# A two-layer trunk in emulated fp32: w_up's product by pairs of pieces in seven block products, w_down by two pieces

## The chip, the core and the metric

One core of a Trainium2 chip runs the whole kernel, one launch. The metric is device time in microseconds; the kernel before takes 1413.79 us, the median of 3 runs (1412.65 to 1416.82).

## What is computed

One inference step of a trunk of two layers: 512 tokens of a new stream and 8 x 16 tokens of running streams, 640 rows of width 1024, all in fp32. Each layer has a mixer (trailing means in the first, forgetting attention in the second) beside memory attention, an output projection, and a squared-ReLU MLP of width 4096, each wrapped in RMS norms. The part that the change touches, for both layers:

```python
h = rmsnorm(x, g_mlp_pre)             # (640, 1024)
u = h @ w_up                          # (640, 4096)
a = jnp.square(jax.nn.relu(u))
x = x + rmsnorm(a @ w_down, g_mlp_post)
```

## The kernel before

TensorE multiplies float32r numbers, and fp32 is emulated: a tensor is split into a high part, rounded to float32r, and the remainder, the low part. A product is then three passes: high by high, high by low, low by high. On weights the split is `piece` (L127 to L138): SyncE fetches 128 x 1024 numbers into a raw buffer, ScalarE (ACT) casts them into `wh` (L136), VectorE (DVE) subtracts to give `wl` (L137). In the input projections GpSimd (POOL) first multiplies the raw piece by a gain (L133). Raw buffers come from a ring of 3, the parts from rings of 8.

The 640 tokens are 5 tiles of 128 in two halves of 384 and 256 columns (`HALF`). `proj_fm` (matmuls of L149) gives one piece of w_up's 128 outputs for one half of the tokens: 8 contraction tiles by 3 passes, 24 matmuls, so 48 a piece, half of 384 and half of 256 columns. `activate` puts ReLU and square on ACT and a square and a subtraction (L469, L470) on DVE. `token_major` (L156, L158, L160) multiplies a token tile by w_down's pieces, two banks of 512 columns, 6 matmuls a piece; DVE adds the banks into `y` (L539). The 32 pieces of a layer go in chunks of 4, 2, 4, 4, 4, 4, 4, 6: up for one chunk lies ahead of down for the one before.

Ahead of the MLP, `OutProj` multiplies the mixed columns by w_out tile by tile; `residual` (L411 to L417) takes the RMS norm of a tile (two squares with sums on ACT, a gain on DVE or POOL, L412, then POOL's power, L166, then DVE's L417), `normed` a second one with its own power (L173, L166, L178 or, without a gain, L176). `flush` transposes that tile on PE (L186) and splits it (L189, L190). A layer's last w_down chunk is followed by the same chain for each tile, and at the end of the second layer by `final_tile`, whose last columns are few.

Each engine runs its instructions in a fixed order that a scheduler sets when the program is built, from the order in which the code is written and from priorities (`flush` has a raised one). An instruction that waits holds up all behind it on its engine, and a DMA that SyncE issues waits for the buffer it fills.

## Time and profile before

| what | value |
|---|---|
| runs | 1412.65, 1413.79, 1416.82 us |
| profiled execution, span | 1411.2 us; its own total is not listed beside it |
| PE busy | 1379.7 us, 98% |
| DVE / ACT / POOL busy | 701.5 / 475.3 / 157.1 us |
| mean granted clock of TensorE | 0.993 |
| w_up pieces, w_down pieces | 64 DMAs of 512 KB each |
| mean DMA rate | 119 GB/s |

Busy times are sums over instructions of the execution. An engine that is busy 98% sets the time; what the others do counts where PE waits for it. Times in a timeline are from the span's start.

### The profile page before, as it was taken

How to read it: one execution, taken by the hardware profiler on the slowest of the kernel's cores; microseconds unless marked ns; L12 is line 12 of the kernel's file. 1: busy time of each engine (PE TensorE's matmuls, PEld its weight loads, DVE VectorE, ACT ScalarE, POOL GpSimd, SP SyncE). 2: the span in 40 equal slices, each digit the busy share in tenths (PEclk: the TensorE clock that was granted, in tenths of full speed). 3: DMA queues.
4: the chain of work that ended last, by engine and by line, in shares of the span. 5: the costliest groups of instructions: out<-in, count | busy, mean ns of one | idle time of the engine just before them, and what ended most of it. 6: DMA issues, size and time to landing. Idle time of an engine off the chain costs nothing. (4 is left out here: it accounts for less than half of the span.)

```text
span 1411.2 us, 20878 instructions
## 1 busy us (share of the span) xinstructions
PE 1379.7 (98%) x8496; PEld 1228.2 (87%) x8496; DVE 701.5 (50%) x1230; ACT 475.3 (34%) x917; POOL 157.1 (11%) x148
## 2 busy tenths in 40 slices
PE   7989999999999999999999999999999999999997
PEld 6988879889889899898999886779898989989896
DVE  6556447454435434445735467557453444434434
ACT  6425335223213223133434345345122322213221
POOL 3270000000000000024511212210000000000003
PEclk9999999999999999999999999999999999999999
DMA  7646565222213212122736533735221322213103
GB/s 258 190 91 210 182 222 194 75 90 90 75 45 105 75 60 90 52 98 105 247 119 222 169 117 104 258 128 198 68 87 55 103 66 71 90 32 119 60 1 120
DMA packets 70034, 167.25 MB, mean 119 GB/s; under 512 B 16545, under 2 KB 24225, under 8 KB 69937
## 3 DMA queue, kind: packets, MB, share of 16 engines
q1 hardware_dynamic: 69936, 165.91, 36.2%
q8 instruction: 67, 1.10, 0.3%
q14 instruction: 31, 0.25, 0.1%
HBM read 148.27 MB, written 17.61 MB: 118 GB/s over the span
## 5 line engine op out<-in xcount | busy, mean ns | idle before, releaser
L136 ACT CAST wh<-raw 128x1024 fp32r<-128x1024 f32 (+1 forms) x180 | 188.2, 1046 | 409.6 <-PE b L160 295.7
L137 DVE TENSOR_TENSOR wl<-raw,wh 128x1024 fp32r<-128x1024 f32 (+1 forms) x180 | 227.1, 1265 | 157.7 <-ACT wh L136 157.6
L149 PE MATMUL b<-hhi,wh 128*128 128x256 f32 (+1 forms) x1336 | 228.8, 313 | 5.9 <-DVE memq L563 5.9
L149 PE MATMUL b<-hhi,wl 128*128 128x256 f32 (+1 forms) x1336 | 226.8, 312 | 0.0
L149 PE MATMUL b<-hlo,wh 128*128 128x256 f32 (+1 forms) x1336 | 222.8, 309 | 0.0
L149 PEld LDWEIGHTS b<-hhi,wh 128*128 128x128 f32 x1336 | 205.2, 189 | 9.6 <-DVE memq L563 6.1
L149 PEld LDWEIGHTS b<-hhi,wl 128*128 128x128 f32 x1336 | 205.0, 190 | 0.3
L149 PEld LDWEIGHTS b<-hlo,wh 128*128 128x128 f32 x1336 | 202.8, 189 | 0.0
L158 PE MATMUL b<-wh,ah 128*128 128x512 f32 x628 | 196.2, 393 | 0.0
L156 PE MATMUL b<-wl,ah 128*128 128x512 f32 x628 | 196.1, 393 | 0.0
L160 PE MATMUL b<-wh,al 128*128 128x512 f32 x628 | 196.0, 393 | 0.0
L539 DVE TENSOR_TENSOR y<-y,b 128x512 f32<-128x512 f32 x138 | 88.7, 683 | 174.6 <-PE b L160 174.6
L160 PEld LDWEIGHTS b<-wh,al 128*128 128x128 f32 x628 | 117.9, 188 | 27.5
L158 PEld LDWEIGHTS b<-wh,ah 128*128 128x128 f32 x628 | 117.9, 188 | 26.9
L467 ACT ACTIVATE r<-b 128x384 f32<-128x384 f32 (+1 forms) x128 | 56.1, 438 | 252.1 <-PE b L149 252.1
L156 PEld LDWEIGHTS b<-wl,ah 128*128 128x128 f32 x628 | 116.9, 188 | 25.5
L469 DVE TENSOR_TENSOR r<-r 128x384 f32<-128x384 f32 (+1 forms) x128 | 62.5, 488 | 109.1 <-ACT ah L468 109.1
L133 POOL TENSOR_TENSOR raw<-raw,gfm 128x1024 f32<-128x1024 f32 (+1 forms) x28 | 56.8, 2031 | 475.2 <-DMA raw<-in_w_in 436.2
L412 POOL TENSOR_TENSOR yn<-y,gp 128x512 f32<-128x512 f32 x18 | 23.0, 1297 | 428.7 <-DVE y L539 424.5
L470 DVE TENSOR_TENSOR al<-r,ah 128x384 fp32r<-128x384 f32 (+1 forms) x128 | 62.9, 491 | 4.3
L468 ACT ACTIVATE ah<-r 128x384 fp32r<-128x384 f32 (+1 forms) x128 | 60.4, 472 | 2.1
L156 PE MATMUL b<-wl,cathi 128*128 128x512 f32 x160 | 54.3, 419 | 0.0
(229 smaller groups left out, 1305.5 us busy)
## 6 DMA issues: line engine op xcount, KB each, us to landing
raw<-in_w_up SPq DMA_DIRECT2D x64, 512.0 KB, 3.8
raw<-in_w_down SPq DMA_DIRECT2D x64, 512.0 KB, 3.2
raw<-in_w_in SPq DMA_DIRECT2D x16, 512.0 KB, 4.5
raw<-in_w_out SPq DMA_DIRECT2D x16, 512.0 KB, 3.6
t<-in_cmk SPq DMA_DIRECT2D x32, 256.0 KB, 6.0
t<-in_cmv SPq DMA_DIRECT2D x32, 256.0 KB, 5.0
x<-xr SPq DMA_DIRECT2D x15, 512.0 KB, 2.7
xr<-x SPq DMA_DIRECT2D x15, 512.0 KB, 4.1
```

Of the source, the lines that this page charges most:

```text
L133: nc.gpsimd.tensor_tensor(out=v, in0=v, in1=gain.unsqueeze(2).to_broadcast([P, n, w // n]), op=ALU.mult)
L136: nc.scalar.copy(out=hi[:, :w], in_=raw[:, :w])
L137: nc.vector.tensor_tensor(out=lo[:, :w], in0=raw[:, :w], in1=hi[:, :w].bitcast(F32), op=ALU.subtract)
L149: nc.tensor.matmul(acc[:, :n], w[:, k, :], x[:, k, :], start=(first and k == 0), stop=(last and k == KT - 1))
L156: nc.tensor.matmul(accs[q][:, :nh], xh, lo[:, c[q]], start=first, stop=False)
L158: nc.tensor.matmul(accs[q][:, :nh], xh, hi[:, c[q]], start=False, stop=False)
L160: nc.tensor.matmul(accs[q][:, :nh], xl, hi[:, c[q]], start=False, stop=last)
L467: nc.scalar.activation(out=r, in_=acc[:, :n], func=AF.Relu)
L468: nc.scalar.activation(out=ah, in_=r, func=AF.Square)
L469: nc.vector.tensor_tensor(out=r, in0=r, in1=r, op=ALU.mult)
L470: nc.vector.tensor_tensor(out=al, in0=r, in1=ah.bitcast(F32), op=ALU.subtract)
L539: nc.vector.tensor_tensor(out=yq, in0=yq, in1=accs[q], op=ALU.add)
```

## The change

Pieces of w_up are taken in pairs (16 a layer). The matrix of weights of a pair (1024 contraction rows, 256 outputs) is cut by halves of the contraction, a pair of pieces being the two halves of the outputs, and the tokens are cut into two halves of 320 (`TH`). The product of these 2 x 2 blocks is made of seven block products (`product`, L547, 12 matmuls of 320 columns each) instead of eight. For that, four sums of weight blocks a pair are taken on POOL (L535 to L538) and split into parts by `parts` (L472, L473), and four sums of token blocks are taken once a layer (`other_blocks`, L500 to L507), of which each is split too. The products are put together with adds on DVE (L562) and two copies on ACT (L554, L559). ReLU and square become one instruction on DVE (L584) on 640 columns.

The token sums need all five tiles; so `flush` leaves raw tokens in `hraw` (copies L463, L465), the first two pairs begin with the two products that need only the raw blocks (`head`, `second`), and their remaining five come behind `other_blocks`, with their w_up pieces of the first half fetched a second time (`load(True)`). w_down goes by two pieces, 14 times, and a last time by four. There are 4 raw buffers instead of 3. The gain of the MLP's norm and the pool of its chain are opened behind the last pair.

```diff
-CHUNKS = (4, 2, 4, 4, 4, 4, 4, 6)
+NPAIR = 16
+TH = 320
...
-    wraw = ctx.enter_context(pool("wraw", 3))
+    wraw = ctx.enter_context(pool("wraw", 4))
...
-            if self.late:
-                tile_to(self.hs, *self.late.pop(0))
+            i, xn = self.late.pop(0)
+            with tc.high_priority(offset=HP):
+                for q in range(2):
+                    acc = bank()
+                    for k in range(4):
+                        nc.tensor.transpose(acc[:, k * P:(k + 1) * P], xn[:, (4 * q + k) * P:(4 * q + k + 1) * P], ident)
+                    dst = self.raw[:, 4 * q:4 * q + 4, i * P:(i + 1) * P]
+                    src = acc.rearrange("p (k t) -> p k t", k=4)
+                    if q == 0:
+                        nc.scalar.copy(out=dst, in_=src)
+                    else:
+                        nc.vector.tensor_copy(out=dst, in_=src)
 
...
-    def mlp(l, proj, x_in, cpool, apool, before, finish):
-        hs = proj.hs
...
-            nc.scalar.activation(out=r, in_=acc[:, :n], func=AF.Relu)
-            nc.scalar.activation(out=ah, in_=r, func=AF.Square)
-            pcs = [piece(a["w_up"][l, f]) for f in fs]
-                    acc = proj_fm(pc, hs[t], n)
+    def split(hi, lo, src):
+        nc.scalar.copy(out=hi, in_=src)
+        nc.vector.tensor_tensor(out=lo, in0=src, in1=hi.bitcast(F32), op=ALU.subtract)
+    def mlp(l, proj, x_in, aside, yside, hst, before, finish):
+        hraw = proj.raw
+        ast, tst, yst = ExitStack(), ExitStack(), ExitStack()
+        apool = ast.enter_context(pool(f"act{l}", 1, aside))
+        tpool = tst.enter_context(pool(f"blk{l}", 1, aside))
+        b1 = (hpool.tile([P, KT, TH], F32R, tag="hi0", name=nm("b1h")), hpool.tile([P, KT, TH], F32R, tag="lo0", name=nm("b1l")))
+        b22 = (hpool.tile([P, 4, TH], F32R, tag="hi1", name=nm("b22h")), hpool.tile([P, 4, TH], F32R, tag="lo1", name=nm("b22l")))
+        ts = [(tpool.tile([P, 4, TH], F32R, name=f"t{x}h_{l}"), tpool.tile([P, 4, TH], F32R, name=f"t{x}l_{l}")) for x in range(4)]
+        b11, b21 = ((b1[0][:, 4 * q:4 * q + 4, :], b1[1][:, 4 * q:4 * q + 4, :]) for q in range(2))
+        def first_blocks():
+            for hi, lo, q in ((*b11, 0), (*b21, 1)):
+                split(hi, lo, hraw[:, 4 * q:4 * q + 4, 0:TH])
+        def other_blocks():
+            r11, r21 = (hraw[:, 4 * q:4 * q + 4, 0:TH] for q in range(2))
+            r12, r22 = (hraw[:, 4 * q:4 * q + 4, TH:2 * TH] for q in range(2))
+            nc.vector.tensor_tensor(out=r11, in0=r12, in1=r11, op=ALU.subtract)
+            split(*b22, r22)
+            nc.gpsimd.tensor_tensor(out=r12, in0=r22, in1=r12, op=ALU.subtract)
+            nc.vector.tensor_tensor(out=r22, in0=r22, in1=r11, op=ALU.subtract)
+            split(*ts[1], r22)
+            split(*ts[2], r12)
+            split(*ts[0], r11)
+            nc.vector.tensor_tensor(out=r21, in0=r21, in1=r22, op=ALU.subtract)
+            split(*ts[3], r21)
+        def parts(src, w=D):
+            hi = wring.tile([P, RW], F32R, tag="wh", name=nm("wh"))
+            lo = wring.tile([P, RW], F32R, tag="wl", name=nm("wl"))
+            split(hi[:, :w], lo[:, :w], src)
+            return [(hi[:, 512 * x:512 * x + 512], lo[:, 512 * x:512 * x + 512]) for x in range(2)]
+        class Pair:
+            def __init__(self, c):
+                self.c = c
+                self.r0 = self.fetch(0)
+                self.a11, self.a12 = parts(self.r0[:, :D])
+            def fetch(self, x):
+                raw = wraw.tile([P, RW], F32, tag="raw", name=nm("raw"))
+                nc.sync.dma_start(out=raw[:, :D], in_=a["w_up"][l, 2 * self.c + x])
+                return raw
+            def load(self, again=False):
+                r0 = self.fetch(0) if again else self.r0
+                r1 = self.fetch(1)
+                s = [wraw.tile([P, RW], F32, tag="raw", name=nm("raw")) for _ in range(2)]
+                s1, s2, s3, s4 = (s[x // 2][:, 512 * (x % 2):512 * (x % 2) + 512] for x in range(4))
+                a11, a12, a21, a22 = (r[:, 512 * x:512 * x + 512] for r in (r0, r1) for x in range(2))
+                nc.gpsimd.tensor_tensor(out=s1, in0=a21, in1=a22, op=ALU.add)
+                nc.gpsimd.tensor_tensor(out=s2, in0=s1, in1=a11, op=ALU.subtract)
+                nc.gpsimd.tensor_tensor(out=s3, in0=a11, in1=a21, op=ALU.subtract)
+                nc.gpsimd.tensor_tensor(out=s4, in0=a12, in1=s2, op=ALU.subtract)
+                self.s1, self.s2 = parts(s[0][:, :D])
+                self.s3, self.s4 = parts(s[1][:, :D])
+                self.a22 = parts(a22, 512)[0]
+            def product(self, w, b, acc, first=True, last=True):
+                w = [x.rearrange("p (k m) -> p k m", k=4) for x in w]
+                for wi, bi, f, e in ((0, 0, first, False), (1, 0, False, False), (0, 1, False, last)):
+                    for k in range(4):
+                        nc.tensor.matmul(acc[:, :TH], w[wi][:, k, :], b[bi][:, k, :], start=(f and k == 0), stop=(e and k == 3),
+                                         skip_group_check=not first)
+            def head(self):
+                self.t = apool.tile([P, 2, 2, TH], F32, tag="c", bufs=2, name=nm("c"))
+                acc = long_bank()
+                self.product(self.a11, b11, acc)
+                nc.scalar.copy(out=self.t[:, 0, 1, :], in_=acc[:, :TH])
+                self.x = acc
+            def second(self):
+                self.product(self.a12, b21, self.x, False, True)
+                nc.scalar.copy(out=self.t[:, 0, 0, :], in_=self.x[:, :TH])
+            def add(self, out, in0, acc):
+                nc.vector.tensor_tensor(out=out, in0=in0, in1=acc[:, :TH], op=ALU.add)
+            def middle(self):
+                c12, c21, c22 = self.t[:, 0, 1, :], self.t[:, 1, 0, :], self.t[:, 1, 1, :]
+                y, w, self.z = bank(), bank(), long_bank()
+                self.product(self.s2, ts[1], y)
+                self.add(c12, c12, y)
+                self.product(self.s3, ts[2], w)
+                self.add(c21, c12, w)
+                self.product(self.s1, ts[0], self.z)
+                self.add(c22, c21, self.z)
+            def end(self):
+                c12, c21 = self.t[:, 0, 1, :], self.t[:, 1, 0, :]
+                v = bank()
+                self.product(self.a22, ts[3], v)
+                self.add(c21, c21, v)
+                self.product(self.s4, b22, self.z, False, True)
+                self.add(c12, c12, self.z)
+                out = [None, None]
+                for x in (1, 0):
+                    t = self.t[:, x].rearrange("p h n -> p (h n)")
+                    nc.vector.scalar_tensor_tensor(out=t, in0=t, scalar=0.0, in1=t, op0=ALU.max, op1=ALU.mult)
+                    out[x] = (apool.tile([P, 640], F32R, tag="ah", bufs=4, name=nm("ah")),
+                              apool.tile([P, 640], F32R, tag="al", bufs=4, name=nm("al")))
+                    split(*out[x], t)
+                return out
+            def whole(self):
+                self.load()
+                self.head()
+                self.middle()
+                self.second()
+                return self.end()
...
-        def down(c, tiles):
+        def down(fs, tiles, first, end):
             nf = len(tiles)
-            end = c == len(CHUNKS) - 1
-            pcs = [piece(a["w_down"][l, f]) for f in chunk(c)]
+            pcs = [piece(a["w_down"][l, f]) for f in fs]
             for i in range(NT):
-                if c == 0:
-                    ys.append(apool.tile([P, D], F32, tag=f"y{i}", name=nm(f"y{i}")))
+                if first:
...
-        ready = up(chunk(0), between=proj.flush)
-        for c in range(len(CHUNKS)):
-            nxt = list(chunk(c + 1)) if c + 1 < len(CHUNKS) else []
-            tiles = up(nxt[:1])
-            if c == 1:
-                gpost.append(gain_tile(cpool, a["g_mlp_post"][l], "gp"))
-            down(c, ready)
-            for f in nxt[1:]:
-                tiles = tiles + up([f])
-            ready = tiles
+        pairs = [Pair(0), Pair(1)]
+        first_blocks()
+        for p in pairs:
+            p.head()
+            p.second()
+        proj.flush()
+        other_blocks()
+        hst.close()
+        ypool = yst.enter_context(pool(f"y{l}", 1, yside))
+        ready = []
+        for p in pairs:
+            p.load(True)
+            p.middle()
+            ready.append(p.end())
+        down((0, 1), ready.pop(0), True, False)
+        for c in range(2, NPAIR):
+            ready.append(Pair(c).whole())
+            if c < NPAIR - 1:
+                down((2 * c - 2, 2 * c - 1), ready.pop(0), False, False)
+        tst.close()
+        cpool = ast.enter_context(pool(f"chain{3 + l}", 2, aside))
+        gpost.append(gain_tile(cpool, a["g_mlp_post"][l], "gp"))
+        down(range(2 * NPAIR - 4, 2 * NPAIR), ready[0] + ready[1], False, True)
+        yst.close()
+        return ast
...
-    nc = bacc.Bacc("TRN2", target_bir_lowering=False, num_devices=1)
+    nc = bacc.Bacc("TRN2", target_bir_lowering=False, num_devices=1, dynamic_dma_scratch_size=1024)
```


**Place 1, the start of a layer.** POOL's queue in layer 0 before, from tile 3's two powers and tile 4's two (`s` is one number a row) on:

```order
L166 TENSOR_TENSOR s_384_2135<-s_383_2133,mhalf 128x1
L166 TENSOR_TENSOR s_388_2146<-s_387_2144,mhalf 128x1
L166 TENSOR_TENSOR s_399_2229<-s_398_2227,mhalf 128x1
L166 TENSOR_TENSOR s_403_2240<-s_402_2238,mhalf 128x1
L133 TENSOR_TENSOR raw_5951<-raw_5951,gfm 128x1024
L133 TENSOR_TENSOR raw_5958<-raw_5958,gfm 128x1024
```

and now, from tile 3's first power through both pairs' sums (`raw_2374` and `raw_2375` hold those of pair 0, `raw_2475` and `raw_2476` those of pair 1) up to tile 4's last power:

```order
L167 TENSOR_TENSOR s_380_2131<-s_379_2129,mhalf 128x1
L535 TENSOR_TENSOR raw_2374<-raw_2372 128x512
L536 TENSOR_TENSOR raw_2374<-raw_2374,raw_2370 128x512
L537 TENSOR_TENSOR raw_2375<-raw_2370,raw_2372 128x512
L167 TENSOR_TENSOR s_384_2142<-s_383_2140,mhalf 128x1
L538 TENSOR_TENSOR raw_2375<-raw_2370,raw_2374 128x512
L535 TENSOR_TENSOR raw_2475<-raw_2473 128x512
L536 TENSOR_TENSOR raw_2475<-raw_2475,raw_2471 128x512
L537 TENSOR_TENSOR raw_2476<-raw_2471,raw_2473 128x512
L167 TENSOR_TENSOR s_395_2223<-s_394_2221,mhalf 128x1
L538 TENSOR_TENSOR raw_2476<-raw_2471,raw_2475 128x512
L167 TENSOR_TENSOR s_399_2234<-s_398_2232,mhalf 128x1
```

Three sums now stand between tile 3's two powers and four more ahead of tile 4's first, where before power stood behind power. The first sum of pair 1 reads `raw_2473`, a piece fetched into the buffer that `raw_2372` held.

ACT's queue at the same place before, from the squares of tile 4 (`jk`) to the first activations:

```order
L411 ACTIVATE jk_2219,s_396_2220<-b_2152 128x512
L136 CAST wh_2616<-raw_2614 128x1024
L411 ACTIVATE jk_2219,s_396_2220<-b_2153 128x512
L136 CAST wh_2622<-raw_2620 128x1024
L467 ACTIVATE r_2303<-b_2278 128x384
L468 ACTIVATE ah_2270<-r_2303 128x384
L173 ACTIVATE xn_2235,s_401_2236<-xr_2216 128x1024
L189 CAST hhi_292_1678<-b_2333 128x4x128
```

and now, from those squares on, up to w_down's first pieces (`c` takes copies of a pair's first products, `wh_2481` and `wh_2485` are casts of pair 1's sums):

```order
L412 ACTIVATE jk_2213,s_392_2214<-b_2148 128x512
L463 COPY hraw_1523<-b_2237 128x4x128
L412 ACTIVATE jk_2213,s_392_2214<-b_2149 128x512
L554 COPY c_2284<-o_2285 128x320
L472 CAST wh_2481<-raw_2475 128x1024
L559 COPY c_2284<-o_2285 128x320
L472 CAST wh_2485<-raw_2476 128x1024
L554 COPY c_2312<-o_2313 128x320
L472 CAST wh_2489<-raw_2473 128x512
L174 ACTIVATE xn_2229,s_397_2230<-xr_2210 128x1024
L559 COPY c_2312<-o_2313 128x320
L137 CAST wh_2574<-raw_2572 128x1024
```

The copy of pair 1's first product, `c_2312` from `o_2313`, stands behind the casts of both of pair 1's sum tiles; PE's next product into `o_2313` waits for that copy.

**Place 2, the end of layer 0.** POOL's queue before, from the last gained piece to the first tile's end (`yn` is a tile's normed output):

```order
L133 TENSOR_TENSOR raw_5979<-raw_5979,gfm 128x1024
L412 TENSOR_TENSOR yn_5611<-y_465_2638,gp_2919 128x512 x2
L166 TENSOR_TENSOR s_876_5622<-s_875_5620,mhalf 128x1
L166 TENSOR_TENSOR s_884_5637<-s_883_5635,mhalf 128x1
L412 TENSOR_TENSOR yn_5682<-y_468_2667,gp_2919 128x512 x2
L166 TENSOR_TENSOR s_893_5693<-s_892_5691,mhalf 128x1
```

and now:

```order
L134 TENSOR_TENSOR raw_6450<-raw_6450,gfm 128x1040
L413 TENSOR_TENSOR yn_5787<-y_0_2584,gp_5731 128x512
L134 TENSOR_TENSOR raw_6457<-raw_6457,gfm 128x1040
L413 TENSOR_TENSOR yn_5787<-y_0_2584,gp_5731 128x512
L167 TENSOR_TENSOR s_1007_5798<-s_1006_5796,mhalf 128x1
L134 TENSOR_TENSOR raw_6464<-raw_6464,gfm 128x1040
L413 TENSOR_TENSOR yn_5846<-y_0_2601,gp_5731 128x512 x2
L167 TENSOR_TENSOR s_1015_5813<-s_1014_5811,mhalf 128x1
L167 TENSOR_TENSOR s_1024_5857<-s_1023_5855,mhalf 128x1
```

Now a gained piece stands between the two halves of the first tile's `yn`, one behind its first power, and the second tile's `yn` ahead of the first one's second power (`s_1015`).

## Rows read from the trace of the kernel before

**Rows 1.** The page's first part: the span, then each engine's busy time, share, instructions.

```profile
span 1411.2 us, 20878 instructions
...
PE 1379.7 (98%) x8496; PEld 1228.2 (87%) x8496; DVE 701.5 (50%) x1230; ACT 475.3 (34%) x917; POOL 157.1 (11%) x148
```

**Rows 2.** PE's waits: who waited for whom, us in total, times, longest.

```profile
PE b L149 <- DVE memq L563: 5.9, 1, 5.9
```

**Rows 3.** The chain of waits, w_up of two chunks: start us, us, what.

```profile
1102.87 28.18 PE b L149 x192
...
1158.84 28.18 PE b L149 x192
```

**Rows 4.** PE's timeline, 72 to 83 us (start us, us, instruction); then the page's part 5.

```profile
72.85 1.07 PE L149 MATMUL b<-hhi,wl 128*128 128x256 f32 x8
...
76.05 1.55 PE L149 MATMUL b<-hhi,wl 128*128 128x384 f32 x8
...
L149 PEld LDWEIGHTS b<-hhi,wl 128*128 128x128 f32 x1336 | 205.0, 190 | 0.3
```

**Rows 5.** Lines by form: minimum, median, maximum ns, first and last start us, shape.

```profile
L137 DVE TENSOR_TENSOR wl<-raw,wh x180: 1204/1225/2937, 26.1 to 1349.3; 128x1024 fp32r<-128x1024 f32 x176, 128x1040 fp32r<-128x1040 f32 x4
...
L412 POOL TENSOR_TENSOR yn<-y,gp x18: 1281/1299/1306, 641.5 to 1397.1; 128x512 f32<-128x512 f32 x18
...
L133 POOL TENSOR_TENSOR raw<-raw,gfm x28: 1890/1926/2418, 22.0 to 806.6; 128x1024 f32<-128x1024 f32 x24, 128x1040 f32<-128x1040 f32 x4
...
L136 ACT CAST wh<-raw x180: 1031/1047/1069, 24.6 to 1348.2; 128x1024 fp32r<-128x1024 f32 x176, 128x1040 fp32r<-128x1040 f32 x4
...
L539 DVE TENSOR_TENSOR y<-y,b x138: 677/680/690, 307.4 to 1395.6; 128x512 f32<-128x512 f32 x138
```

**Rows 6.** Timelines of DVE and POOL, 74 to 84 and 640 to 652 us.

```profile
74.66 6.48 DVE L137 TENSOR_TENSOR wl<-raw,wh 128x1024 fp32r<-128x1024 f32 x3
...
75.51 2.13 POOL L133 TENSOR_TENSOR raw<-raw,gfm 128x1024 f32<-128x1024 f32 x1 [2.07 <-ACT u L604]
...
80.14 2.35 POOL L667 TENSOR_TENSOR s<-s 128x781 f32<-128x781 f32 x1
...
642.99 1.10 DVE L414 TENSOR_TENSOR s<-s 128x1 f32<-128x1 f32 x1 [0.95 <-ACT jk L411]
...
641.52 2.55 POOL L412 TENSOR_TENSOR yn<-y,gp 128x512 f32<-128x512 f32 x2 [0.92 <-DVE y L539]
```

**Rows 7.** Timelines at the start of layer 0's MLP: PE, POOL, then DVE.

```profile
225.96 1.57 PE L149 MATMUL b<-hhi,wh 128*128 128x384 f32 x8
...
220.99 1.46 POOL L166 TENSOR_TENSOR s<-s,mhalf 128x1 f32<-128x1 f32 x1 [3.86 <-DVE s L164]
...
222.48 1.28 DVE L178 SCALAR_TENSOR_TENSOR xn<-xr,s,gq 128x1024 f32<-128x1024 f32 x1 [0.44 <-POOL s L166]
...
230.98 0.15 DVE L414 TENSOR_TENSOR s<-s 128x1 f32<-128x1 f32 x1
...
236.03 1.28 DVE L178 SCALAR_TENSOR_TENSOR xn<-xr,s,gq 128x1024 f32<-128x1024 f32 x1 [0.44 <-POOL s L166]
```

**Rows 8.** PE's timeline, 91 to 109 us; then stretches: busy us by engine, granted clock, DMA.

```profile
101.67 2.93 PE L149 MATMUL b<-hhi,wh 128*128 128x384 f32 x8 [5.92 <-DVE memq L563]
...
102.00:105.00 3.00, 3.00 (x10) 3.00 (x10) 3.00 (x6) 0.00 (x0) 0.00 (x0) 0.50 0.26 57
```

**Rows 9.** DVE's timeline at the end of layer 0's MLP, 640 to 652 us.

```profile
640.75 1.28 DVE L539 TENSOR_TENSOR y<-y,b 128x512 f32<-128x512 f32 x2 [4.72 <-PE b L160]
...
648.38 0.75 DVE L176 TENSOR_SCALAR xn<-xr,s 128x1024 f32<-128x1024 f32 x1 [0.66 <-POOL s L166]
```

**Rows 10.** DVE's timeline at the end of the kernel, 1393 to 1411 us.

```profile
1395.03 1.28 DVE L539 TENSOR_TENSOR y<-y,b 128x512 f32<-128x512 f32 x2 [2.65 <-PE b L160]
...
1399.29 1.41 DVE L417 SCALAR_TENSOR_TENSOR xr<-yn,s,xr 128x512 f32<-128x512 f32 x2 [0.66 <-POOL s L166]
```

**Rows 11.** DMA issues: KB each, median us from issue to landing.

```profile
raw<-in_w_up SPq DMA_DIRECT2D x64, 512.0 KB, 3.8
```

More of the change, by code (lines that the diff above doesn't have):

```diff
@@ L424, in __init__, with open @@
             self.l, self.cat, self.x_in, self.name, self.pcs, self.order = l, cat, x_in, name, pcs, order
-            self.hs, self.x_out, self.late = None, [], []
-        def open(self, cpool):
-            self.cpool = cpool
+            self.x_out, self.late = [], []
+        def open(self, cpool, raw):
+            self.cpool, self.raw = cpool, raw
             self.gpost = gain_tile(cpool, a["g_mix_post"][self.l], "gp")
@@ L535, in down @@
                     yq = ys[i][:, q * 512:(q + 1) * 512]
-                    if c == 0:
+                    if first:
                         nc.vector.tensor_copy(out=yq, in_=accs[q])
@@ L710, in trunk_kernel, with raw_tokens @@
     mst.close()
+    def raw_tokens(side, l):
+        st = ExitStack()
+        return st, st.enter_context(pool(f"hraw{l}", 1, side)).tile([P, KT, 2 * TH], F32, name=f"hraw{l}")
+    hst, hraw = raw_tokens("right", 0)
     st1 = ExitStack()
@@ L734, in before0 @@
             tile_to(hs1, *late.pop(0), HALF1, 0)
-    with ExitStack() as s:
-        mlp(0, proj, proj.x_out, cpool, s.enter_context(pool("mlp0", 1)), before0, finish0)
+    st1.close()
+    st1 = mlp(0, proj, proj.x_out, "left", "right", hst, before0, finish0)
     hs = hs1
@@ L1108, in trunk_kernel @@
     fox.close()
+    hst, hraw = raw_tokens("left", 1)
     st2 = ExitStack()
     cpool = st2.enter_context(pool("chain2", 2))
-    proj.open(cpool)
+    proj.open(cpool, hraw)
     drive(sampp, Dense(tiles))
```

36 lines of the change are left out of this document (11 added, 25 removed).

## The prediction

> **What bounds the kernel now.** The page's first part comes first: TensorE (PE) is busy 1379.7 of 1411.2 us, 98% [rows 1], so only 31.5 us of the span are without a matmul. The list of PE's waits says how little of that is anything the other engines do: the longest wait for another engine is 5.9 us, in the first projection [rows 2]. Then the chain of waits, in order of time: through both MLPs it is a row of equal stretches, 192 matmuls of L149 in 28.18 us, the next one 55.96 us later [rows 3]; the 27.78 us between are the w_down tiles. VectorE (DVE) is busy half the time, ScalarE a third, POOL a ninth [rows 1]. So fewer matmuls shorten the kernel one for one, unless the operands now come late.
>
> **What the change takes away.** One matmul of w_up takes 28.18/192 = 0.1468 us at a mean of 320 columns [rows 3], which is the width of the new ones. A pair of pieces had 96, and has 7 x 12 = 84; over 32 pairs 384 matmuls go: 384 x 0.1468 = **-56.4 us**, all on PE. w_down keeps its matmuls: by two pieces a tile takes half of what it took by four.
>
> **A pair in the middle of a layer.** Its period is 84 x 0.1468 + 60 x 0.2315 = 26.2 us (0.2315 is 27.78 us over the 120 w_down matmuls of four pieces). DVE does in it five and a half splits of 128x1024 at 1.23 (6.8 us), ten adds into y at 0.68 (6.8), five adds of 320 columns (about 0.45 by width: 2.3), two multiplications and two splits of 640 (about 0.8 each: 3.2): 19 us. POOL does four sums of 128x512 at 1.30, 5.2 us [rows 5]. Weights are prepared one pair ahead, DVE's adds stand between matmuls of another bank, and even DVE and POOL laid end to end make 24.3 of 26.2. I take **0**. The bound below is 0; above, about 1 us in each of 28 pairs, 28 us, if the slack of 1.9 breaks at the joints. y is now added into 150 times a layer, not 80: that lies inside these 19 us.
>
> **The start of a layer.** Before, the first w_up matmul starts at 225.96, where the output projection's last one ends [rows 7]. Now PE needs, one behind the other in the fixed order: tile 3's transposes inside tile 4's product, pair 0's two block products, pair 1's two, tile 4's transposes, and then token sums of all five tiles. I walked the five queues with the durations of the rows, each instruction waiting for its inputs and for the one ahead of it. The waits of PE come out so, first if POOL and DVE never hinder each other, then if every instruction with two SBUF inputs on the one holds up the other:
> - Tile 3: POOL's power (L166, then at 220.99 [rows 7]) now stands behind three sums, 3 x 1.30 [rows 5]; xn moves from 222.5 [rows 7] to about 224 or 226.6. PE waits 0.7, or 3.1; then 1.0, or 0.6, for the split of the second half.
> - **Pair 1's second piece.** Four raw buffers: its fetch takes the one that pair 0's second piece held, and waits for DVE's remainder of a22, which on DVE stands behind tile 4's two yn, at 234, or 236.3. Landing 3.8 us [rows 11], sums s1, s2, s3, the power, s4 (4 x 1.30 + 0.55), a cast of 1.05 [rows 5], and only then, by ACT's order, the copy (about 0.45) that the last block product of pair 1's start waits for: 236.3 + 3.8 + 5.8 + 1.05 + 0.45 = 247.4, with DVE's split of 1.2 in between 248.6. PE has run its 36 matmuls by 235.7: it waits **11.4, or 12.9**.
> - Tile 4: its power is behind those three sums too, so xn, then ready at 237.3 [rows 7], comes at about 249 or 252.4: PE waits 2.0.
> - Token sums: one subtraction, one cast and one split of 1280 columns (about 1.5, 1.3 and 1.5 us, by width from [rows 5]) five times over, with w_down's first two pieces ahead on DVE: PE waits 6.2, or 6.5, before t0, and then 3.2, or 10.8, in five waits while the splits keep pace or not.
>
> The sums are 24.5 and 35.9 us a layer. Which end? One DVE instruction of 0.15 us [rows 7] took 1.10 while POOL worked on yn from 641.52, and ended with it; three splits beside POOL's work from 75.51 to 82.49 took 6.48, not 3.7 [rows 6, 5]: held up 2.8 in some 5.6 us of overlap. The one is full exclusion, the other half; I take three quarters of the way, **33 us**. Layer 1 starts by the same order in all five queues: 2 x 33 = **+66 us**, bounds 49 and 72.
>
> The Trainium skill speaks against the change here: SBUF — State Buffer, section "SBUF: two separate sides", says that POOL and a DVE instruction with two SBUF inputs share a pair of ports which one of them holds for its whole instruction while the other blocks. By that rule the starts cost the upper end, 72 for both layers, and the time would be 6 us above mine; the 2.8 of 5.6 us of the three splits is the row here that does not agree with it in full.
>
> **TensorE's clock.** After the 5.9 us without a matmul the granted clock was 0.50, 1.2 GHz, in 102 to 105, and 8 matmuls took 2.93 us [rows 8], not 1.55 [rows 4]: 1.4 us lost there and some 0.6 behind it. The two long waits of a start will do the same, but most of that time lies ahead of further waits. I add 1 us a layer, **+2**; bounds 0 and 8.
>
> **End of layer 0.** The last w_down tiles have 4 pieces now, 5.6 us each (27.78 / 5), where they had 6, 8.3 us. From a tile's last product to its xn it is 640.75 to 649.1, 8.4 us [rows 9]. POOL now has a gained piece (L134, 1.93 [rows 5]) between the tile's two yn, and the next tile's yn ahead of its second power, so xn comes some 11 us after. Tiles that come every 5.6 us no longer hide that: I take **+3.5 us** before the first transposes; 0 if they are far enough behind, 8 if each tile waits.
>
> **Tail.** Behind tile 3's product DVE is taken until 1400.7 [rows 10] with that tile's residual; the last tile's product now takes 5.6 us, not 8.4, so it waits for DVE: of the 2.8 us, **+2** come back (0 to 3). The two refetched pieces a layer, 512 KB at 3.8 us, cost nothing of their own beyond the start's waits; the wider scratch setting nothing.
>
> **Sum:** -56.4 + 66 + 2 + 3.5 + 2 + 0 = +17.1. On the profiled execution's 1411.2 this gives 1428.3. Its own total is not shown beside the span; the median of the runs is 1413.8, 2.6 above it (0.2%), and I lay that on top: 1430.9, said as **1430 us**.
>
> **Rivals.**
> - *The queues give way at the start (faster).* If pair 1's second piece is not held up, by a buffer that comes free earlier than I read, the 11.4 to 12.9 us and tile 4's 2.0 go, and 11 to 21 us a layer stay; with 12, -56.4 + 24 + 5.5 = -27, **1387 us** (5.5 is the end of layer 0 and the tail; waits this short have no fallen clock behind them). For it: before, not one wait at a start. Against: the order shows the sums and the power in one queue. It decides below 22 us a layer: -56.4 + 44 + 7.5 is -4.9, over 0.3% faster. Chance 0.18.
> - *No hindrance between POOL and DVE.* The lower end, 24.5 twice: -56.4 + 49 + 7.5 = 0, **1414 us**. Against: the 1.10 us for an instruction of 0.15. Chance 0.15.
> - *The middle breaks.* Where a pair's sums, a split and an add meet, PE waits 1 us in each of 28 pairs: **1458 us**; 0.5 us gives 1444. For it: 24.3 of 26.2 us. Against: work is one pair ahead. Chance 0.14.
> - *The saving isn't there.* If a matmul of 320 columns took what one of 384 takes, because its weight load of 0.190 us [rows 4] sets the pace, a pair would cost 84 x 0.174 = 14.6, not 14.1, and the time would be above 1500. Against: 8 matmuls of 256 columns take 1.07 us, with the same loads [rows 4]. Chance 0.02.
> - *Full exclusion.* The upper end, 35.9 twice: -56.4 + 72 + 7.5 = +23, **1437 us**. For it: the 1.10 us, which ended with POOL's instruction. Against: the three splits. Chance 0.16. (It is what the Trainium skill's page above would have.)
> - My forecast, half to three quarters of an exclusion, 1420 to 1433: 0.35.
>
> **How the numbers follow.** About 0.3% (4.2 us) is what a measurement of this kernel can tell from no change. Faster takes 0.17 of the first rival and a share of the second, 0.05: 0.22. Same, 1409.6 to 1418: the rest of the second and the lower edge of the forecast, 0.13. Slower: what is left of the forecast, full exclusion, the middle that breaks and the saving that isn't there, 0.65. The range of 8 in 10 runs from 1392, with two thirds of the first rival left out, to 1448, with the upper half of the breaking middle and the absent saving left out.
>
> **What would show it.** Right: PE without a wait in the pairs, 84 matmuls a pair in 12.3 us where 96 took 14.1; at each start a wait of 11 to 13 us whose releaser is ScalarE's copy (L554), one of about 6 us before t0 (L547 for ts[0]), and a granted clock of 0.5 behind them; PE's waits over the span about 31.5 + 70. Wrong: starts under 21 us in all, waits that recur in every pair, or matmuls of 320 columns that take more than 0.15 us.

## The result, and the profile after

The changed kernel takes **1425.5 us** (median of 4 runs, 1422.84 to 1427.95) against 1413.22 for the kernel before in the same session: ratio 1.0082, interval 1.0061 to 1.0102. It is slower, inside the range and 4.5 us under the forecast of 1430. The profiled execution has a span of 1425.2 us, 14.0 above that of before [rows 1]. The forecast's sum came out nearly right because two of its terms were wrong in opposite directions, as the rows below show.

The page of the changed kernel: the span, busy time by engine, and the adds into y.

```profile
span 1425.2 us, 20624 instructions
...
PE 1348.5 (95%) x8106; PEld 1188.9 (83%) x8106; DVE 967.6 (68%) x1476; ACT 505.8 (35%) x857; POOL 352.3 (25%) x278
...
L649 DVE TENSOR_TENSOR y<-y,b 128x512 f32<-128x512 f32 x278 | 177.1, 680 | 44.0 <-PE b L161 43.1
```

PE is busy 31 us less than in [rows 1], and idle 76.7 us instead of 31.5. The 278 adds into y are twice those of [rows 5], at the same 680 ns. PE's waits, in the columns of [rows 2]:

```profile
PE o L547 <- ACT c L554: 12.9, 2, 7.2
PE o L547 <- ACT t0h L472: 10.5, 2, 5.4
PE b L150 <- DVE memq L689: 7.2, 1, 7.2
PE b L187 <- DVE xn L177: 6.9, 2, 4.0
...
PE b L459 <- DVE xn L179: 5.5, 4, 2.6
PE o L547 <- DVE t0l L473: 3.5, 2, 1.7
```

The two longest are the two that the prediction named, ScalarE's copy and the first token sum, once a layer each. The wait for `memq` lies in the first projection, ahead of both MLPs. By stretches (us; then busy us of PE, PEld, DVE, ACT and POOL with the instructions in brackets, granted clock, DMA share, GB/s), first the middles of the two layers, then the two starts:

```profile
280.00:620.00 340.00, 340.00 (x1872) 306.11 (x1871) 253.41 (x327) 105.19 (x132) 73.19 (x52) 1.00 0.24 81
1010.00:1380.00 370.00, 370.00 (x2037) 333.14 (x2036) 277.56 (x360) 113.81 (x142) 73.05 (x52) 1.00 0.24 80
220.00:280.00 60.00, 39.76 (x213) 35.52 (x212) 50.85 (x49) 25.69 (x34) 26.48 (x16) 0.86 0.27 91
920.00:1010.00 90.00, 73.53 (x421) 59.41 (x418) 60.47 (x81) 39.13 (x69) 35.85 (x27) 0.83 0.32 111
```

In the middle PE is never without work: 340.00 of 340 us and 370.00 of 370. One pair there is 84 matmuls from 291.86 to 304.19, 12.33 us or 0.1468 each, as taken:

```profile
291.86 0.75 PE L547 MATMUL o<-b1h,wh 128*128 128x320 f32 x4
...
304.19 0.63 PE L157 MATMUL b<-wl,ah 128*128 128x512 f32 x2
```

Nearly all the loss is at the joints. The start of layer 0's MLP in PE's timeline (`xn` is a normed tile):

```profile
226.19 0.33 PE L459 MATMUL b<-idt,xn 128*128 128x128 f32 x1 [2.55 <-DVE xn L179]
...
241.10 1.43 PE L547 MATMUL o<-b1h,wh 128*128 128x320 f32 x4 [7.17 <-ACT c L554]
242.33 1.27 PE L547 MATMUL o<-b1h,wl 128*128 128x320 f32 x4
...
244.89 1.53 PE L459 MATMUL b<-idt,xn 128*128 128x128 f32 x8 [0.22 <-DVE xn L179]
251.81 1.44 PE L547 MATMUL o<-t0h,wh 128*128 128x320 f32 x4 [5.39 <-ACT t0h L472]
...
256.06 1.44 PE L547 MATMUL o<-t0l,wh 128*128 128x320 f32 x4 [1.74 <-DVE t0l L473]
...
259.83 0.85 PE L547 MATMUL b<-t1h,wh 128*128 128x320 f32 x4 [0.47 <-ACT t1h L472]
...
263.51 0.85 PE L547 MATMUL b<-t1l,wh 128*128 128x320 f32 x4 [1.95 <-DVE t1l L473]
...
267.30 0.85 PE L547 MATMUL b<-t3h,wh 128*128 128x320 f32 x4 [0.74 <-ACT t3h L472]
...
276.20 0.63 PE L157 MATMUL b<-wl,ah 128*128 128x512 f32 x2
```

**What a start costs.** From the end of the matmul ahead of the first wait (223.64) to the first w_down matmul (276.20) are 52.56 us. PE has in them 156 matmuls of L547 (22.9 us at 0.1468; one block product of 12 lies behind), 16 transposes (2.1) and the last 5 matmuls of the output projection (1.2): 26.1. So the start costs **26.5 us**: 20.2 of waits, and 6.2 that is left, most of it matmuls at half clock (four in 1.27 us at 242.33, usually 0.75; the granted clock was 0.50 from 241.0 to 244.6). The same stretch of layer 1, 965.70 to 1019.07, gives **27.3**.

The second piece of pair 1 is fetched when VectorE's split of pair 0's first two sums ends (VectorE's row, then SyncE's):

```profile
228.06 1.21 DVE L473 TENSOR_TENSOR wl<-raw,wh 128x1024 fp32r<-128x1024 f32 x1
...
229.29 0.33 SPq L526 DMA_DIRECT2D raw<-in_w_up  x1
```

**What holds the operands up** is in the timelines of VectorE, then POOL, at this start:

```profile
250.39 1.49 DVE L473 TENSOR_TENSOR b22l<-hraw,b22h 128x1280 fp32r<-128x1280 f32 x1
251.80 4.20 DVE L473 TENSOR_TENSOR t0l<-hraw,t0h 128x1280 fp32r<-128x1280 f32 x1
255.93 2.56 DVE L503 TENSOR_TENSOR hraw<-hraw 128x1280 f32<-128x1280 f32 x1
...
260.89 2.56 DVE L473 TENSOR_TENSOR t1l<-hraw,t1h 128x1280 fp32r<-128x1280 f32 x1
...
222.03 1.28 POOL L537 TENSOR_TENSOR raw<-raw,raw 128x512 f32<-128x512 f32 x1
...
250.54 4.11 POOL L502 TENSOR_TENSOR hraw<-hraw 128x1280 f32<-128x1280 f32 x1 [7.12 <-DVE hraw L500]
254.62 2.52 POOL L535 TENSOR_TENSOR raw<-raw 128x512 f32<-128x512 f32 x1
...
259.58 2.52 POOL L536 TENSOR_TENSOR raw<-raw,raw 128x512 f32<-128x512 f32 x1
```

A split of 1280 columns takes 1.49 us on VectorE, and a sum of 128x512 takes 1.28 on POOL (at 222.03). Here each takes 2.5 to 2.6, on both engines, with the same period. From start to start, splits without POOL beside them are 1.41 us apart (250.39 to 251.80) and sums without VectorE 1.25 (222.03 to 223.28), 2.66 together; here both are 2.48 apart. The two engines take turns for nearly all of their time. The first `t0l` is the clearest: POOL's token sum ends at 254.65, and the split that was issued at 251.80 ends at 256.00, 1.35 later. Neither row shows a wait; the time in which an engine is locked out counts as its busy time. At each start pair 2's four weight sums, whose product begins only at 291.86, some 30 us later, thus take over two fifths of VectorE's time in this stretch, while PE waits for its splits.

**End of layer 0.** PE's timeline from the last w_up matmul on, then VectorE's, then PE at layer 1's memory attention:

```profile
645.01 0.63 PE L157 MATMUL b<-wl,ah 128*128 128x512 f32 x2
...
667.26 1.97 PE L187 MATMUL b<-idt,xn 128*128 128x128 f32 x8 [3.97 <-DVE xn L177]
668.88 1.20 PE L157 MATMUL b<-wl,ah 128*128 128x512 f32 x2
...
653.85 1.28 DVE L649 TENSOR_TENSOR y<-y,b 128x512 f32<-128x512 f32 x2 [2.06 <-PE b L161]
656.08 1.73 DVE L415 TENSOR_TENSOR s<-s 128x1 f32<-128x1 f32 x1 [0.95 <-ACT jk L412]
...
666.46 0.75 DVE L177 TENSOR_SCALAR xn<-xr,s 128x1024 f32<-128x1024 f32 x1 [2.42 <-POOL s L167]
...
720.65 1.02 PE L280 MATMUL b<-mk1r,memq 128*128 128x256 f32 x4
```

The same two places in the kernel before:

```profile
632.45 0.62 PE L156 MATMUL b<-wl,ah 128*128 128x512 f32 x2
...
710.85 1.03 PE L279 MATMUL b<-mk1r,memq 128*128 128x256 f32 x4
```

They are 75.64 us apart now. Before they were 78.40, of which 13.89 belong to 60 more w_down matmuls (the last chunk had six pieces, not four; 0.2315 each): 64.5 for the same work, so this stretch costs **11.1 us**.

From the add into y to xn are 13.4 us (653.85 to 667.2), where they were 8.4 [rows 9]. One subtraction of 128x1 takes 1.73 us beside POOL's gained piece, usually 0.15 [rows 7].

### The profile page after: what moved, and what is told of

Its sections match the earlier page's. It is cut to its first block, busy times and chain, and to the rows that moved or that the text cites. A ratio compares the mean times of both kernels' runs of the same rounds, so it can differ in the third digit from the quotient of the medians.

```text
span 1425.2 us, 20624 instructions
## 1 busy us (share of the span) xinstructions
PE 1348.5 (95%) x8106; PEld 1188.9 (83%) x8106; DVE 967.6 (68%) x1476; ACT 505.8 (35%) x857; POOL 352.3 (25%) x278
## 5 line engine op out<-in xcount | busy, mean ns | idle before, releaser
L472 ACT CAST wh<-raw 128x1024 fp32r<-128x1024 f32 (+1 forms) x128 | 120.4, 942 | 410.5 <-PE b L161 244.2
L649 DVE TENSOR_TENSOR y<-y,b 128x512 f32<-128x512 f32 x278 | 177.1, 680 | 44.0 <-PE b L161 43.1
L473 DVE TENSOR_TENSOR wl<-raw,wh 128x1024 fp32r<-128x1024 f32 (+1 forms) x128 | 140.2, 1098 | 66.5 <-ACT wh L472 66.5
L138 DVE TENSOR_TENSOR wl<-raw,wh 128x1024 fp32r<-128x1024 f32 (+1 forms) x116 | 172.4, 1490 | 15.3 <-ACT wh L137 15.1
L535 POOL TENSOR_TENSOR raw<-raw 128x512 f32<-128x512 f32 x32 | 46.0, 1439 | 511.9 <-DMA raw<-in_w_up 314.7
L137 ACT CAST wh<-raw 128x1024 fp32r<-128x1024 f32 (+1 forms) x116 | 121.5, 1049 | 133.1 <-PE b L150 48.0
L134 POOL TENSOR_TENSOR raw<-raw,gfm 128x1024 f32<-128x1024 f32 (+1 forms) x28 | 56.4, 2021 | 124.9 <-issue 48.3
L562 DVE TENSOR_TENSOR c<-c,b 128x320 f32<-128x320 f32 x96 | 46.7, 486 | 50.0 <-PE b L547 47.7
L472 ACT CAST ah<-c 128x640 fp32r<-128x640 f32 x64 | 46.6, 729 | 52.6 <-DVE c L584 52.6
L150 PE MATMUL b<-hhi,wh 128*128 128x384 f32 (+1 forms) x312 | 55.8, 321 | 7.2 <-DVE memq L689 7.2
L547 PE MATMUL o<-b1h,wh 128*128 128x320 f32 x256 | 50.2, 320 | 12.9 <-ACT c L554 12.9
L473 DVE TENSOR_TENSOR al<-c,ah 128x640 fp32r<-128x640 f32 x64 | 60.6, 950 | 0.8 <-ACT ah L472 0.8
L536 POOL TENSOR_TENSOR raw<-raw,raw 128x512 f32<-128x512 f32 x32 | 56.7, 1773 | 2.4
L547 PEld LDWEIGHTS o<-b1h,wh 128*128 128x128 f32 x256 | 42.5, 194 | 16.2 <-ACT c L554 13.8
L150 PEld LDWEIGHTS b<-hhi,wh 128*128 128x128 f32 x312 | 48.2, 192 | 9.2 <-DVE memq L689 7.4
```

Of the source, the lines that this page charges most:

```text
L134: nc.gpsimd.tensor_tensor(out=v, in0=v, in1=gain.unsqueeze(2).to_broadcast([P, n, w // n]), op=ALU.mult)
L137: nc.scalar.copy(out=hi[:, :w], in_=raw[:, :w])
L138: nc.vector.tensor_tensor(out=lo[:, :w], in0=raw[:, :w], in1=hi[:, :w].bitcast(F32), op=ALU.subtract)
L150: nc.tensor.matmul(acc[:, :n], w[:, k, :], x[:, k, :], start=(first and k == 0), stop=(last and k == KT - 1))
L472: nc.scalar.copy(out=hi, in_=src)
L473: nc.vector.tensor_tensor(out=lo, in0=src, in1=hi.bitcast(F32), op=ALU.subtract)
```

## The experiments

Each was timed beside the kernel before, whose median in these sessions was 1413.9 to 1415.1.

**plain2: the first two pairs of a layer by eight block products.** They need no sums of tokens or weights and no second fetch, at the price of 12 matmuls a pair, 48 in all (+7.0 us on PE).

```diff
+        class Plain(Pair):
+            def half(self, h):
+                b = ((b11, b21), (ts[3], b22))[h]
+                for x in range(2):
+                    acc = bank()
+                    self.product(self.a[x][0], b[0], acc, True, False)
+                    self.product(self.a[x][1], b[1], acc, False, True, True)
+                    nc.scalar.copy(out=self.t[:, x, h, :], in_=acc[:, :TH])
...
-        pairs = [Pair(0), Pair(1)]
+        pairs = [Plain(0), Plain(1)]
```

> The first two pairs of each layer by eight block products, without weight sums, refetch or token sums; the other fourteen by seven. If the 27 us that PE loses at each start come from the first pairs' need of sums, 24 more matmuls a layer cost 3.5 us, some 3 us of waits stay, and the time is 1425.5 - 2 x 27 + 2 x 6.5 = 1384 us (1376 to 1393), faster than before. Rival: the waits only move to the first w_down tiles, which need the space of the raw tokens; then 1405 to 1425.

Measured: 1396.02 us (1391.9 to 1399.87), ratio to before 0.987 [0.9844, 0.9896]. 29 us under the change with 7.0 us of matmuls more: some 36 of the 54 us that the two starts cost came back, so the starts are where the change's gain went. It missed the expected 1384 for two waits that remained (PE's waits of this kernel):

```profile
PE b L459 <- DVE xn L179: 8.4, 2, 4.4
...
PE b L550 <- DVE b22l L473: 4.2, 2, 2.1
```

Tile 4's power stands behind pair 2's sums in POOL's queue, and the split of b22 took 4.23 us beside a POOL sum of 4.06.

**w5: a fifth raw buffer** (the scratch `jk` in bfloat16 makes room), so that pair 1's second piece comes earlier.

```diff
-    wraw = ctx.enter_context(pool("wraw", 4))
+    wraw = ctx.enter_context(pool("wraw", 5))
...
-        jk = cpool.tile([P, 512], F32, tag="jk", bufs=1, name=nm("jk"))
+        jk = cpool.tile([P, 512], mybir.dt.bfloat16, tag="jk", bufs=1, name=nm("jk"))
```

> Five raw buffers instead of four (and the scratch output of one square in half the bytes, to make room). If PE's wait for ScalarE's copy (7.2 and 5.7 us) comes from pair 1's second piece waiting for a raw buffer, and tile 4's power behind pair 1's sums, both come some 5 us earlier: 1425.5 - 10 = 1415 us (1411 to 1418), and the wait for the copy falls below 2 us. Rival: what comes after it, the token sums, is late by itself and takes up the gain; then 1421 to 1426.

Measured: 1428.1 us (1426.69 to 1428.9), 1.0096 [1.008, 1.0113]: no gain, and 2 us above the rival's range. The piece did come earlier (its first sum began 12.0 us behind tile 3's residual, in the change 16.8), but PE's wait for the copy did not fall: 13.0 us in all, in four waits. The rival had looked for the loss in the token sums, behind the copy. In ScalarE's timeline:

```profile
234.68 1.04 ACT L472 CAST wh<-raw 128x1024 fp32r<-128x1024 f32 x1 [4.91 <-POOL raw L536]
...
237.42 0.42 ACT L554 COPY c<-o 128x320 f32<-128x320 f32 x1
```

The cast of pair 1's sums, which waits for POOL, moved ahead of tile 4's squares and of the copy. With four buffers and with five, what PE waits for stood behind POOL's sums.

**nosum2: pair 2 without its four sums.** Raw blocks of weights stand in their place. This shows what the sums cost beside the token sums.

```diff
-                nc.gpsimd.tensor_tensor(out=s1, in0=a21, in1=a22, op=ALU.add)
...
+                if self.c == 2:
+                    s = [r1, r0]
+                else:
+                    nc.gpsimd.tensor_tensor(out=s1, in0=a21, in1=a22, op=ALU.add)
...
```

> Pair 2 of each layer without its four weight sums (raw weight blocks stand in their place in three of its products); nothing else changes. If POOL and DVE shut each other out, DVE's four instructions of 1280 columns beside these sums fall from 2.56 to 1.47 us and each layer's start gains 4 us: 1417 us (1415 to 1420). Rival: they are slow for another reason, or off the path; then 1424 to 1426.

Measured: 1420.2 us (1415.66 to 1421.25), 1.0035 [1.0021, 1.005], 5.3 below the change and at the upper edge of what was expected. Beside these sums four VectorE instructions of 1280 columns took 2.56 to 2.58 us each, with nothing beside them they take 1.48 or 1.49; the first of the four:

```profile
252.38 1.48 DVE L503 TENSOR_TENSOR hraw<-hraw 128x1280 f32<-128x1280 f32 x1
```

So it is POOL's work that held them up. The waits for t1l, t1h and t3h are gone, those for the copy (15.5) and t0h (11.0) are not. Eight instructions whose results are wanted some 30 us later were worth about 5 us.

**late: pairs 0 and 1 may not start their second set of sums before tile 4 is normed.** It takes the sums out of the way of the powers and the copies.

```diff
+            self.last = xn
...
+                if again:
+                    for x in s:
+                        nc.vector.tensor_copy(out=x[:, 0:1], in_=proj.last[:, 0:1])
```

> The changed kernel with one thing moved: the weight sums of pairs 0 and 1 of each layer may not begin before tile 4's normed output is there (one column of their tiles is first written from it). POOL's powers then stand ahead of them, and no cast of a sum stands ahead of ScalarE's copies. If this order is what PE waits for, the wait for the copy (7.2 and 5.7 us) and the ones for tile 3 (2.6 us) go, tile 4 is ready 6 us earlier, the sums and splits move behind it, and 5 to 7 us a layer are gained: 1413 us (1408 to 1417). Rival: the sums and splits are simply too much work ahead of the first seven-product pairs, wherever they stand; then 1421 to 1428.

Measured: 1427.82 us (1424.59 to 1428.12), 1.0089 [1.0063, 1.0116]. My theory of a queue order fell here. The wait for the copy went down to 1.4 us in all, and this came in its place:

```profile
PE b L551 <- ACT t1h L473: 29.1, 2, 15.6
```

So it is not one instruction in the wrong place: the sums and splits take their time wherever they stand. That they do so because the two engines take turns this run does not show; the next one bears on it.

**dvesum: the sums of the first three pairs on VectorE instead of POOL**, which follows from the two before: if they take turns, a sum costs both 1.28 us on POOL and 0.68 on VectorE.

```diff
-                nc.gpsimd.tensor_tensor(out=s1, in0=a21, in1=a22, op=ALU.add)
-                nc.gpsimd.tensor_tensor(out=s2, in0=s1, in1=a11, op=ALU.subtract)
...
+                eng = nc.vector if self.c < 3 else nc.gpsimd
+                eng.tensor_tensor(out=s1, in0=a21, in1=a22, op=ALU.add)
+                eng.tensor_tensor(out=s2, in0=s1, in1=a11, op=ALU.subtract)
...
```

> The change, with the weight sums of the first three pairs of each layer on VectorE instead of POOL (24 instructions of 128x512 in all). My theory: at a layer's start POOL and VectorE work one at a time, so that a sum costs both engines its whole 1.28 us on POOL, and 0.68 on VectorE (what an add of 128x512 takes there): 0.6 us less for each of 12 sums a layer, and the powers that ScalarE and VectorE wait for are no longer behind sums in POOL's queue. I expect 4 to 8 us less a layer, 1413 us (1409 to 1418). Rival: the two engines overlap for most of their time, so that POOL's sums were nearly free; then VectorE gets 12 x 0.68 = 8.2 us more a layer in the queue that PE waits for, and the time is 1430 to 1437.

Measured: **1406.33 us** (1402.91 to 1407.12), ratio to before 0.9935 [0.9914, 0.9956]; it turns the change from slower to faster by moving 24 instructions to another engine, and by more than I expected. PE's timeline at layer 0's start, then VectorE's and POOL's:

```profile
230.54 0.86 PE L548 MATMUL o<-b1h,wh 128*128 128x320 f32 x4 [0.52 <-ACT c L555]
235.93 1.39 PE L459 MATMUL b<-idt,xn 128*128 128x128 f32 x8 [3.35 <-DVE xn L179]
241.50 1.43 PE L548 MATMUL o<-t0h,wh 128*128 128x320 f32 x4 [4.18 <-ACT t0h L472]
246.15 1.43 PE L548 MATMUL o<-t0l,wh 128*128 128x320 f32 x4 [2.15 <-DVE t0l L473]
...
240.50 4.20 DVE L473 TENSOR_TENSOR b22l<-hraw,b22h 128x1280 fp32r<-128x1280 f32 x1
244.61 1.48 DVE L473 TENSOR_TENSOR t0l<-hraw,t0h 128x1280 fp32r<-128x1280 f32 x1
...
239.52 3.82 POOL L502 TENSOR_TENSOR hraw<-hraw 128x1280 f32<-128x1280 f32 x1 [5.06 <-DVE hraw L500]
```

VectorE has more to do and every split is back at 1.48 us, but for the one beside the only sum left to POOL (L502), which takes 4.20. The copy that PE waited 7.17 us for now costs 0.52 here. The waits before tile 4's transposes and for t0 are most of what is left. Two things changed at once: the splits are no longer held up, and the sums ahead of the copy and of the powers are shorter and out of POOL's queue. The run does not part them; nosum2 shows the first alone. Together the two leave no room for the rival that POOL's sums were nearly free.

**two: the kernel before with w_down by two pieces**, the other half of the change, alone (`CHUNKS` also sets how many pieces of w_up stand between).

```diff
-CHUNKS = (4, 2, 4, 4, 4, 4, 4, 6)
+CHUNKS = (4,) + (2,) * 12 + (4,)
```

> The kernel before, with w_down by 4, then twelve times 2, then 4 pieces, w_up unchanged: the w_down part alone. If the shorter last tiles uncover the chain at the end of layer 0 and the tail, it costs 7.6 + 2.5 + 1.6 = some 10 us: 1423 us (1419 to 1426). Rival: those waits come with the other parts (POOL's sums, later gains); then 1412 to 1416.

Measured: 1422.68 us (1419.18 to 1423.74), 1.0062 [1.0043, 1.0081], +8.8. The part of the change that I thought nearly free costs most of what the whole loses. Its profiled execution was its fastest, span 1416.5, 5.3 above that of before; the other 3 or 4 us are not seen in a profile. It shows 5.2 us of waits for xn of L176, the longest 3.5, where the kernel before has one of 1.2. From the last w_up matmul to layer 1's memory attention it takes 72.3 us (642.62 to 714.91), 7.8 more than the 64.5, and the tail behind PE's last matmul is 9.7 us, not 7.6.

**vec: the gain of the last chunk's `residual` on VectorE**, in both layers.

```diff
-                    residual([ys[i][:, :512], ys[i][:, 512:]], cpool, gpost[0], xr, nc.gpsimd)
+                    residual([ys[i][:, :512], ys[i][:, 512:]], cpool, gpost[0], xr, nc.vector)
```

> The changed kernel with the gain of a tile's normed output (yn, L413, at the end of both MLPs) on VectorE instead of POOL. If POOL's two yn, the gained pieces between them and their exclusion of VectorE make the chain at the end of layer 0 late, its waits of PE fall from 7.6 us (with the clock) to 1 or 2 and the tail by 1: 1418 us (1415 to 1421). Rival: the chain is late by its other members; then 1424 to 1427.

Measured: 1418.56 us (10 runs, 1415.4 to 1421.5), 1.003 [1.0015, 1.0045], 7 below the change, as expected; the waits are not: the first transposes wait 1.11 us, not 3.97, but one of 3.5 stays in the next projection (3.0 in the change). By the profiles 2.2 us come back between the last w_up matmul and layer 1's memory attention (73.45 instead of 75.64) and 2.0 in the tail (7.2 instead of 9.2); where the rest of the 7 lies is open. So POOL's place in the chain is a part of what the end of layer 0 costs, and not the most of it.

**spin28: idle matmuls in the two long waits.** It adds to the change 28 matmuls of 320 columns before pair 1's second product and 7 in fp32 before the token sums, whose results nobody reads, to hold the clock.

```diff
+        def spin(w, rhs, n):
+            acc = bank()
+            for j in range(n):
+                nc.tensor.matmul(acc[:, :TH], w[:, 0:128], rhs, start=j == 0, stop=j == n - 1)
...
+            if p.c == 1:
+                spin(p.a12[0], b1[0][:, 0, :], 28)
...
+        spin(ident, hraw[:, 0, TH:2 * TH], 7)
```

> The changed kernel with idle work on PE at each layer's start: 28 matmuls of 320 columns into an unread bank before pair 1's second product, 7 of fp32 ahead of the token sums, so that the granted clock stays up. If the matmuls at 1.2 GHz (some 45 in each start, 5 us) lengthen the kernel, it gains about 4 us a layer: 1417 us (1414 to 1420). If they lie ahead of waits for ScalarE and VectorE, as the prediction has it, the clock stays up and the time stays: 1424 to 1428.

Measured: 1426.11 us (1424.21 to 1429.85), 1.0091 [1.0058, 1.0125], with a mean granted clock of 0.979 to 0.982, in the change 0.971 to 0.975. Fewer slow matmuls, and not faster: most of them lie ahead of the next wait, which takes up what they give. The clock still fell in part (8 transposes at 242.06 took 1.94 us), so what the slow matmuls that are left cost stays open.

**best4 and best6: the parts together.** best4 is plain2 with vec's edit, all token sums on VectorE, and pair 2's weight sums held until b22 is split; best6 takes pair 2's weight sums to VectorE as well, as in dvesum. The token sums are also taken in another order.

```diff
-            nc.gpsimd.tensor_tensor(out=r12, in0=r22, in1=r12, op=ALU.subtract)
+            nc.vector.tensor_tensor(out=r12, in0=r22, in1=r12, op=ALU.subtract)
+            nc.vector.tensor_tensor(out=r11, in0=r12, in1=r11, op=ALU.add)
...
+                if self.c == 2:
+                    for x in s:
+                        nc.vector.tensor_copy(out=x[:, 0:1], in_=b22[1][:, 0, 0:1].bitcast(F32))
```

> The first two pairs by eight block products, as in the run plain2, the token sums on VectorE alone and in an order that leaves the second token block's split first, pair 2's weight sums not before that split, and yn at the end on VectorE. If what is left in plain2 is tile 4's power behind POOL's sums (4.4 and 3.9 us), the split b22 behind POOL's token sum (2.1 and 2.0 us) and the end of layer 0, it goes: 1396 - 12 - 6 = 1380 us (1376 to 1386). Rival: VectorE, with more work in the start, delays the first w_down tiles; then 1390 to 1397.

> The combined version (two pairs by eight block products, the gain of the last chain on VectorE, token sums on VectorE) with pair 2's weight sums on VectorE too, before 1385.75 without this. My theory: pair 2's four sums cost 4 x 0.6 us less of the two engines' shared time a layer; what PE waited for there was 3.7 us a layer for the first additions into y, so at most that comes back: 1382 us (1378 to 1386). Rival: the four sums (2.7 us) now stand in VectorE's own queue ahead of the adds that PE waits for, and the time is 1388 to 1392.

Measured: best4 1385.75 us (1384.8 to 1386.7), 0.9797 [0.9773, 0.9821]; best6 **1380.96 us** (1379.55 to 1383.99), 0.9764 [0.9746, 0.9782], the fastest, 2.4% under the kernel before. In best4 PE still waited 7.4 us in all for the first adds into y; in best6 that is 1.2, and its starts have one wait over a microsecond in layer 0:

```profile
238.59 0.33 PE L459 MATMUL b<-idt,xn 128*128 128x128 f32 x1 [1.87 <-DVE xn L179]
```

## Why the prediction was right, term by term

| term | predicted us | in the profiled execution |
|---|---|---|
| 384 matmuls fewer | -56.4 | -56.4 (84 matmuls of a pair in 12.33) |
| middle | 0 | 0 (340.00 busy of 340) |
| two starts, with the fallen clock | +68 | +53.8 (26.5 and 27.3) |
| end of layer 0 | +3.5 | +11.1 |
| tail | +2 | +1.6 |
| not in the sum | | -1.3 ahead of the starts, +2.5 in layer 1's attention, +1.7 in layer 0, not placed |
| sum | +17.1 | +13.0; the spans differ by 14.0 |

Layer 1's memory attention starts at 720.65 and started at 710.85 in the kernel before, +9.8; arriving 1.3 early, -28.2 for half of the matmuls, +26.5 for the start and 11.1 for the end of layer 0 leave 1.7 that is not placed. The tail is the time from PE's last matmul to the end of the span, 7.6 us before and 9.2 now. The +2.5 in the attention of layer 1 stays open: its waits differ by tenths of a microsecond, and no run was made for it.

- **The saving and the middle** were right, and with them two rivals fell: no wait recurs in a pair, and 320 columns take 0.1468 us.
- **The start: right mechanism, too large, for the most part by one misreading.** The step that failed is "its fetch takes the one that pair 0's second piece held, and waits for DVE's remainder of a22". The fetch was issued at 229.3, when VectorE's split of pair 0's first two sums ended (228.06 + 1.21), so it had their buffer, 5 to 7 us before the time I used. In the built program `raw_2473` has the address of `raw_2374`, not that of `raw_2372`; so what is said with the change, that it went into the buffer that `raw_2372` held, is wrong too. So the copy came after 7.17 and 5.68 us, not 11.4 or 12.9, and tile 4 cost 0.22 and not 2.0. These two are 7 us a start too many in the forecast, about what the 34 us (33 and 1 for the clock) are too large against 26.5. The other terms agree only in sum: tile 3, t0 and the waits behind t0, with the clock, were 19.5 us in the forecast, and came to 12.8 of waits and 6.2 of slow matmuls. The rival in which the queues give way went too far the other way: the piece landed earlier, but its four sums, a power and a cast still stood ahead of the copy.
- **Half or full exclusion: nearly full, and my row said so.** I read three splits in 6.48 us beside "some 5.6 us" of POOL's work as a hold-up of one half. But POOL's rows there are stretched as well: its three instructions took 2.13, 2.47 and 2.35 us, and the same ones take 1.90, 1.49 and 1.49 elsewhere in that part of the trace. Of the 5.6 us only some 3.5 were POOL's own work, and 2.8 of hold-up are four fifths of that. Setting held-up time against the other engine's *busy* time counts the waiting twice. The rows of the changed kernel show the same: a period of 2.48, where turns without any overlap would make 2.66. The Trainium skill, SBUF — State Buffer, section "SBUF: two separate sides", says that of the two the first holds the shared ports for its whole instruction and the other blocks; this trace agrees (a split that stood 2.85 us beside one POOL instruction and ended 1.35 behind it, where it takes 1.49 alone), and dvesum, which acts on it, is 19 us faster than the change. The rule of the Trainium skill's page held; the 1437 that I worked out beside it rests on the later landing above as well, and 7.5 of the 10.4 us that each of its starts has too many (35.9 and 1 for the clock, against 26.5) lie there.
- **The clock** was right in that most of its cost lies ahead of further waits: some 6 us of a start are slow matmuls, where 1 was added, but the time was 1426.11 against 1425.5 with fewer of them. They took the place of waits: the five behind t0, 3.2 or 10.8 us in the forecast, came to 4.9 and 2.9. They are not to be added to the waits that follow them.
- **End of layer 0: mis-sized, 11.1 and not 3.5.** The mechanism was named (gained pieces on POOL between the two yn, tiles that come every 5.6 us). I priced one wait. There were two, 3.97 and 3.0, one of 1.2 for `ah`, matmuls at half clock behind each, and VectorE's own small instructions held up beside POOL (1.73 us for 0.15); the chain took 13.4 us and not some 11. The run two, with nothing of w_up's change, shows 7.8 of the 11.1, and vec gives back 2.2: the shorter last tiles are the larger part, POOL's pieces the smaller. best6 still takes 73.6 us for this stretch, 9 above the 64.5.
- **Tail:** 1.6 for 2.
- **The signs named ahead:** the two waits and their releasers came, but the copy's was 7.17 and 5.68 us, not 11 to 13, and PE is idle 76.7 us, not about 101.

So "slower" was right for the reason given: late operands at the starts eat the 56 us. But the forecast's 1430 owes its closeness to luck: 14 us too many at the starts, against some 8 too few at the end of layer 0 and 3 that no term had.

## What to carry to other kernels

A matmul scheme that saves TensorE's time by sums on other engines has its price at the joints, where the sums cannot be hidden: use the plain product for the first pieces there, and the scheme in the middle (2.4% faster instead of 0.8% slower here). When VectorE and POOL work beside each other on SBUF operands, add their own times up, and put an operation where it is shortest, even if that engine is the busier one. Look up which buffer a fetch takes in the built program rather than in the order of the code: one buffer misread put the forecast's landing 5 to 7 us late. And an earlier landing by itself gained nothing (w5).
